# A router's load requests and its VectorE and ScalarE instructions put in one written order

## The chip, the cores and the metric

The kernel runs on one core of a Trainium2 chip. A core has TensorE (PE), VectorE (DVE), ScalarE (ACT), GpSimd (POOL) and SyncE (SP), each with an instruction queue of its own; SP issues nearly all of the loads here. The metric is the device time of one execution in microseconds (us), shown as the median of several runs.

## The reference, cut to what matters

One transformer block on 512 tokens of width 1024, in float32: a mixer (mLSTM and forgetting attention), a cross-attention on 256 memory rows, and a mixture of 32 experts in 4 groups, two experts for each token. Then a norm.

```python
x = x + merged @ w_out[l]
x = x + _cross_attention(_rmsnorm(x, g_xq[l]), _rmsnorm(mem, g_xmem[l]), w_xq[l], w_xkv[l], w_xo[l])
x = x + _hier_moe(_rmsnorm(x, g_moe[l]), w_rg[l], b_rg[l], w_re[l], b_re[l], w_gate[l], w_up[l], w_down[l])
```

Inside `_hier_moe` a token's logits pick a group and, in it, the best two experts; each expert is `silu(t @ w_gate) * (t @ w_up) @ w_down`, weighted and summed. The 32 experts hold 192 MiB of weights, all of which are read.

## The kernel before, in words

The change lies between the last attention head and the first pair of experts.

**w_xo.** The cross-attention's output product goes over four column blocks c of 256 columns. Each block needs two loads of 512 KB (`load_w`, L111 to L126): a request on SP into a buffer `wraw` (three of them), then a rounded high part `wh` on ACT (L124) and a rest `wl` on DVE (L125). Blocks 0 and 1 run in and right behind the last head (L642 to L657). Blocks 2 and 3 are `rw2` and `rw3` (L663); their four loads are the fifth to eighth of w_xo. A token block of theirs (`of_block`, L181) is 24 matmuls (12 with the first load, 12 with the second) and an add into the residual x (L525). In `ROUT` (L46), `x0` to `x3` are the token blocks of rw2 and `p0` to `p3` those of rw3.

**The router.** The other words of ROUT are its steps, the digit being a token block of 128 (or a half of two blocks for C, K and G): `t` transposes x on PE and copies it on ACT (L753), `l` multiplies it by the router's weights (L762), `s` and `r` sum squares on ACT (L766) and make the reciprocal root on DVE and POOL (L771, L772, L99), `Xh` and `Xl` write the high part of the scaled tokens on ACT (L780) and the low part on DVE (L782), `g` scales the logits (L788), `C` picks the experts on DVE (L797 to L818), `K` counts places with matmuls (L827) and then makes slots and hit tables on DVE (L830 to L837, L733, L734), and `G` gathers the first pair's tokens with matmuls (L883).

**The experts.** 16 pairs; for each, `stationary` gathers the tokens of 64 slots an expert (L1018, L1020), `gate_up` (L1043) multiplies by gate and up, `down` (L1067) by the third weight, `combine` (L1093, L1094) adds the results to x. The weights come in 192 pieces of 1 MB in a ring of 14 buffers (`RING`), nine of them named m; `h` and `l` take the places of `wh` and `wl`, and `r` lies in memory that is free when the router is done. `experts.load(n)` asks for all pieces up to n.

**What sets the order.** A scheduler orders each queue by a simulated clock. Inside `tc.manual_schedule(engines=...)` the instructions of the named engines keep the order in which they are written; those of other engines, and those of another such block, may be put between. In the kernel before, one block (L664) fixes PE, DVE and ACT from the loads of rw2 through the last word of ROUT. SP is in none. `experts.load(9)` stands behind the four loads of w_xo, and `experts.load(NAHEAD)` (11) at the word `v`. Behind that, PE is fixed in a block over all pairs (L1104); the two `st` tiles of the first pair (L1106) are in a DVE and ACT block of their own, and `codes`, `numbers` and `weight_parts` (the table of slots, the token numbers and the weights of the slots; L841 to L875, L964 to L978) in another (L1114).

Of the kernel before, what the change touches and what calls it, by code (L numbers as in the profile page):

```python
# [42 lines left out]
NAHEAD = 11  # L43


ROUT = ("x0 t00 t01 v s0 p0 l00 t02 s1 r0 x1 l01 t03 X0 p1 t10 l02 s2 r1 x2 l03 l10 t11 X1 s3 p2 l11 r2 g0 g1 C0 x3 t12 "  # L46
        "X2h K0 p3 X2l l12 t13 r3 l13 g2 g3 C1 G0 X3h K1 X3l G1")
NR = 8 + NE

C_MLQ, C_MLK, C_MLV, C_MLO = 0, 512, 1024, 2048  # L50
# [8 lines left out]
def emit(ctx, tc, a):  # L59
# [4 lines left out]
    dram = ctx.enter_context(tc.tile_pool(name="dram", bufs=1, space=bass.MemoryType.DRAM))  # L64
    accp = ctx.enter_context(tc.tile_pool(name="accp", bufs=4, space=PSUM))
    attp = ctx.enter_context(tc.tile_pool(name="attp", bufs=2, space=PSUM))
    small = ctx.enter_context(tc.tile_pool(name="small", bufs=8))
# [10 lines left out]
    def left(name, bufs=1):  # L78
        return tc.tile_pool(name=name, bufs=bufs, side="left", reuse_waits="tile")

    def right(name, bufs=1):
        return tc.tile_pool(name=name, bufs=bufs, side="right", reuse_waits="tile")


    ident = consts.tile([P, P], F32, name="ident")
# [21 lines left out]
    wp = None  # L107
# [20 lines left out]
    def drain(g):  # L128
        for _ in g:
            pass  # L130
# [97 lines left out]
    wp = ctx.enter_context(left("wp"))  # L228
# [269 lines left out]
    X1 = [X1a[:, tb] for tb in range(NB)]  # L498
# [17 lines left out]
    r2 = ExitStack()  # L516
# [5 lines left out]
    def resid_rows(src, hs, hl_, c):  # L522
        def ev(tb, n, ps):
            x = X1a[:, tb:tb + n, c * 256:(c + 1) * 256]
            V.tensor_add(x, x, ps)  # L525
        return Rows(src, c * 256, hs, hl_, NB, ev)
# [49 lines left out]
    with right("xa") as xa, tc.manual_schedule(engines={mybir.EngineType.PE}):  # L576
# [3 lines left out]
        def q_proj(hd, qs):  # L580
            def eq(i, ps):
                h = xa.tile([P, T], F32R, name="xqh", tag="xqh", bufs=4)
                l = xa.tile([P, T], F32R, name="xql", tag="xql", bufs=4)
                split(h, l, ps)
                qs.append((h, l))
            return proj_cols_g(a["w_xq"], hd * 256, xh, xl, T, eq)
# [51 lines left out]
        for hd in range(XA_H):  # L638
            nq = []
            if hd < XA_H - 1:  # L640
                g, per = q_proj(hd + 1, nq), 1
            else:  # L642
                def first_halves():
                    for c in range(2):
                        rows_o.append(resid_rows(a["w_xo"], oth, otl, c))
                        yield from rows_o[c].half(0)
                g, per = first_halves(), 2
# [12 lines left out]
    mraw = ctx.enter_context(right("mraw"))  # L660
    wx[:] = [0, s_ot.enter_context(left("wx"))]
    router, experts = moe(ctx, tc, a, X1, dram, small, acc, pss, pso, left, right, ident, rpow, wp, rt_, mraw, wx[1])
    rw2, rw3 = (resid_rows(a["w_xo"], oth, otl, c) for c in (2, 3))  # L663
    with tc.manual_schedule(engines={mybir.EngineType.PE, mybir.EngineType.DVE, mybir.EngineType.Activation}):  # L664
        rw2.loads()
        rw3.loads()
        experts.load(9)
        for w in ROUT.split():
            n = [int(x) if x.isdigit() else x for x in w[1:]]
            if w == "v":  # L670
                experts.load(NAHEAD)
            elif w[0] in "xp":
                drain((rw2 if w[0] == "x" else rw3).of_block(n[0]))
            else:
                router[w[0]](*n)
    s_ot.close()
    experts.run()


def router_consts(ctx, nc, a, left, gcol):  # L680
# [211 lines left out]
class Experts:  # L892
# [52 lines left out]
    def rows(self, e, w):  # L945
        return [*self.got[e, w, 0], *self.got[e, w, 1]]

    def run(self):
        self.mr2 = self.ctx.enter_context(self.right("mr2"))
        run_experts(self, *self.args)  # L950


def run_experts(ex, ctx, tc, a, X2, dram, small, acc, pss, pso, left, right, ident, rpow, wp, c, mraw):
    nc = tc.nc
    V, S, G, TE, SP = nc.vector, nc.scalar, nc.gpsimd, nc.tensor, nc.sync
    iot, iot64, Eb, Ab, rk, tokf, wsl = c.iot, c.iot64, c.Eb, c.Ab, c.rk, c.tokf, c.wsl
# [7 lines left out]
    def weight_parts():  # L964

        wpt = c.wparts
        dn = sg.tile([P, NB], F32, name="dn")
        V.scalar_tensor_tensor(dn, c.dv, 1.0, c.gs, op0=OP.add, op1=OP.mult)
        V.reciprocal(wf[:, :, 0], dn)
        V.tensor_mul(wf[:, :, 1], wf[:, :, 0], c.dv)  # L970
        rem = sg.tile([P, NB, 2], F32, name="rem")
        V.tensor_copy(wpt[:, :, :, 0], wf)
        V.tensor_sub(rem, wf, wpt[:, :, :, 0])
        V.tensor_copy(wpt[:, :, :, 1], rem)
        V.tensor_sub(rem, rem, wpt[:, :, :, 1])
        V.tensor_copy(wpt[:, :, :, 2], rem)
        V.tensor_mul(Vw, Eb.rearrange("p b j e -> p (b j) e")[:, :, None, :].to_broadcast([P, 2 * NB, 3, NE]),
                     wpt.rearrange("p b j a -> p (b j) a")[:, :, :, None].to_broadcast([P, 2 * NB, 3, NE]))  # L978
# [32 lines left out]
    def stationary(G_, g, n=P, pt=None):  # L1011

        st = sg.tile([P, 4, n], F32, name="st", tag="st", bufs=4)
        if pt is None:
            pt = pss()
            for j in range(4):
                for i in range(2 * NB):
                    TE.matmul(pt[:, j * n:(j + 1) * n], c.XN[:, i % 2, i // 2, (4 * g + j) * P:(4 * g + j + 1) * P],  # L1018
                              G_[:, i // 2, :n], start=i == 0, stop=i == 2 * NB - 1)
        V.tensor_mul(st, pt[:, :4 * n].rearrange("p (j t) -> p j t", j=4),  # L1020
                     c.gsc[:, 4 * g:4 * g + 4, None].to_broadcast([P, 4, n]))
        return st

    def slots_of(p):
        G_ = sg.tile([P, NB, P], F16, name="G", tag="G", bufs=2)
        for tb in range(NB):
            for i in range(2):
                e = 2 * p + i
                G.tensor_scalar(G_[:, tb, i * 64:i * 64 + 64], iot[:, :64], c.code[:, tb, e:e + 1], None,  # L1029
                                op0=OP.is_equal)  # L1030
        return G_
# [4 lines left out]
    def gate_up(sts, ws, ps):  # L1036


        for ph in range(2):
            for k in range(KB):  # L1040
                for h, w in enumerate(ws):
                    i = (ph + h) % 2
                    TE.matmul(ps[i][half(h)], sts[k // 4][:, k % 4, half(h)], w[i][k], start=k == 0, stop=k == KB - 1)  # L1043
                yield
# [36 lines left out]
    def places(tokcol, k=P):  # L1081
        C = sg.tile([P, T], F32R, name="C", tag="C", bufs=2)
        G.tensor_scalar(C[:k], iot[:k], tokcol, None, op0=OP.is_equal)
        return C
# [13 lines left out]
    def advance(g, n=99):  # L1098
        for _ in range(n):
            if g is None or next(g, "end") == "end":  # L1100
                return

    ex.load(len(ex.order))
    with tc.manual_schedule(engines={mybir.EngineType.PE}):  # L1104
        with tc.manual_schedule(engines={mybir.EngineType.DVE, mybir.EngineType.Activation}):
            sts = [stationary(c.G0, g, pt=c.pts[g]) for g in range(2)]  # L1106
        before = None
        for p in range(NPAIR):
            es = (2 * p, 2 * p + 1)
            ps = [acc(), acc()]  # L1110
            gu = gate_up(sts, [(ex.rows(e, 0), ex.rows(e, 1)) for e in es], ps)
            if p == 0:
                advance(gu, 6)
                with tc.manual_schedule(engines={mybir.EngineType.DVE, mybir.EngineType.Activation}):  # L1114
                    for f in (c.codes, c.numbers):
                        for h in range(2):
                            f(h)
                    weight_parts()
            if p + 1 < NPAIR:
                G_ = slots_of(p + 1)  # L1120
            C = places(tokf[:, p:p + 1])
            advance(gu, 4 if p else 2)
            cb = None
            if before:
                hT = turned(before[0], P)
            advance(gu, 4 if p else 0)
            if before:
                o = [pso(), pso()]
                advance(down(hT, [ex.rows(e, 2) for e in before[1]], o))
                cb = combine(*weigh(o, wsl[:, p - 1:p]), before[2])  # L1130
            advance(gu, 4)
            if p == 0:
                weights()
            if p == 1:
                nt, inc, nov = counts()
            nst = []
            if p + 1 < NPAIR:
                nst.append(stationary(G_, 0))
            advance(gu, 2)
            advance(cb, 4)  # L1140
            advance(gu, 2)
            if p + 1 < NPAIR:
                nst.append(stationary(G_, 1))
            advance(cb, 4)
            before = act(ps, P), es, C
            sts = nst
        hT = turned(before[0], P)
        o = [pso(), pso()]
        advance(down(hT, [ex.rows(e, 2) for e in before[1]], o))
        C = before[2]  # L1150
# [5 lines left out]
    with tc.If(n_ov > 0):  # L1156
        with left("ov") as ov:
# [4 lines left out]
            for tb in range(NB):  # L1162
                for j in range(2):
# [3 lines left out]
                    r1 = rk[:, tb, j:j + 1]  # L1167
# [42 lines left out]
            with tc.For_i(0, n_ov, 1) as it:  # L1210
                e = nc.values_load(ei[0:1, bass.ds(it, 1)], min_val=0, max_val=NE - 1,
                                   engines=[mybir.EngineType.SP])
# [17 lines left out]
    for tb in range(NB):  # L1230
# [3 lines left out]
        v = small.tile([P, 1], F32, name="vv", tag="vv")  # L1234
# [49 lines left out]
```

## Time and profile before

| | us |
|---|---|
| median of 3 runs (1303.69 to 1304.48) | 1303.83 |
| the profiled execution, its own time | 1306.05 |
| its span, first to last instruction | 1304.30 |
| mean granted clock of TensorE over the span | 0.988 |

Times in the rows are us from the start of the span. In a timeline a row is the start, the length, the engine, the line and operation, the tile written and those read, the shape and the count; in square brackets stands how long the engine was idle before it, and what ended that. SPq is SP's queue of requests. The length of a matmul is that of one pass through the pipeline, and matmuls overlap, so their rate is read from their starts. "x24" is a row of 24 instructions put together.

### The profile page before, as it was taken

How to read it: one execution, taken by the hardware profiler on the slowest of the kernel's cores; microseconds unless marked ns; L12 is line 12 of the kernel's file. 1: busy time of each engine (PE TensorE's matmuls, PEld its weight loads, DVE VectorE, ACT ScalarE, POOL GpSimd, SP SyncE). 2: the span in 40 equal slices, each digit the busy share in tenths (PEclk: the TensorE clock that was granted, in tenths of full speed). 3: DMA queues.
4: the chain of work that ended last, by engine and by line, in shares of the span. 5: the costliest groups of instructions: out<-in, count | busy, mean ns of one | idle time of the engine just before them, and what ended most of it. 6: DMA issues, size and time to landing. Idle time of an engine off the chain costs nothing.

```text
span 1304.3 us, 18633 instructions
## 1 busy us (share of the span) xinstructions
PE 1253.0 (96%) x7606; PEld 900.9 (69%) x7606; DVE 552.6 (42%) x1045; ACT 355.7 (27%) x627; POOL 132.3 (10%) x250
## 2 busy tenths in 40 slices
PE   6999999999999999999999986999999999999996
PEld 6898999888888977899978985444444444444443
DVE  4437455334566654446555516232323222222325
ACT  4435344222344442325434333000000000000102
POOL 0001011000001010001000003111112211111001
PEclk9999999999999999999999988999999999999998
DMA  4352422344344325233521444999999999999971
GB/s 167 85 111 82 81 90 74 96 97 89 89 86 84 88 82 159 83 130 120 178 81 50 191 164 180 403 417 418 419 417 418 418 418 414 417 417 416 418 326 66
DMA packets 99114, 278.45 MB, mean 213 GB/s; under 512 B 6197, under 2 KB 67909, under 8 KB 77905
## 3 DMA queue, kind: packets, MB, share of 16 engines
q1 hardware_dynamic: 97536, 272.46, 58.1%
q0 software_dynamic: 1488, 4.76, 1.1%
q8 instruction: 61, 1.00, 0.3%
q14 instruction: 29, 0.23, 0.1%
HBM read 275.08 MB, written 2.12 MB: 213 GB/s over the span
## 4 chain that ended last, share of the span: by engine, by line
PE 91%; DVE 4%; DMA 2%; ACT 1%; issue 1%; SPq 1%; POOL 0%; POOLq 0%; ACTq 0%; DVEq 0%
PE acc L1043 18%; PE acc L103 16%; PE acc L104 16%; PE acc L105 16%; PE pso L1067 8%; PE pss L1018 4%; PE pss L1093 1%; DMA wraw<-w_xo 1%; PE pso L1094 1%; PE pso L1093 1%; PE pss L103 1%; DVE wl L125 1%; PE pss L105 1%; PE pss L104 1%; PE pss L1056 1%
## 5 line engine op out<-in xcount | busy, mean ns | idle before, releaser
L1043 PE MATMUL acc<-mw,st 128*64 128x512 f32 x880 | 238.0, 604 | 0.4 <-DVE st L1020 0.4
L125 DVE TENSOR_TENSOR wl<-wraw,wh 128x1024 fp32r<-128x1024 f32 x120 | 146.9, 1224 | 193.7 <-ACT wh L124 189.1
L124 ACT ACTIVATE wh<-wraw 128x1024 fp32r<-128x1024 f32 x120 | 126.8, 1058 | 202.8 <-PE acc L104 93.2
L1043 PEld LDWEIGHTS acc<-mw,st 128*64 128x64 f32 x880 | 67.6, 138 | 109.7 <-issue 104.5
L103 PE MATMUL acc<-hH,wh 128*128 128x512 f32 x320 | 128.3, 401 | 0.0
L104 PE MATMUL acc<-hL,wh 128*128 128x512 f32 x320 | 127.8, 399 | 0.0
L105 PE MATMUL acc<-hH,wl 128*128 128x512 f32 x320 | 126.0, 401 | 1.7 <-DVE wl L125 1.7
L1078 DVE SCALAR_TENSOR_TENSOR yl<-pso,wsl,yh 128x512 fp32r<-128x512 f32 x32 | 22.5, 746 | 225.4 <-ACT yh L1077 225.4
L1067 PE MATMUL pso<-mw,hT 128*64 128x512 f32 x440 | 112.6, 592 | 0.7 <-ACT hT L1058 0.7
L104 PE MATMUL acc<-wl,hH 128*128 128x256 f32 x384 | 109.5, 286 | 1.1 <-DVE wl L125 1.1
L103 PE MATMUL acc<-wh,hH 128*128 128x256 f32 x384 | 109.6, 287 | 0.5 <-ACT wh L124 0.5
L105 PE MATMUL acc<-wh,hL 128*128 128x256 f32 x384 | 109.3, 285 | 0.2 <-DVE hL L196 0.2
L1029 POOL TENSOR_SCALAR G<-iot,code 128x64 f16<-128x64 f32 x120 | 52.9, 468 | 317.7 <-PE pss L1018 312.5
L1067 PEld LDWEIGHTS pso<-mw,hT 128*64 128x64 f32 x440 | 37.2, 137 | 61.4 <-issue 59.7
L104 PEld LDWEIGHTS acc<-wl,hH 128*128 128x128 f32 x384 | 73.3, 191 | 1.9 <-DVE wl L125 1.6
L103 PEld LDWEIGHTS acc<-wh,hH 128*128 128x128 f32 x384 | 73.0, 190 | 1.3 <-ACT wh L124 0.9
L105 PEld LDWEIGHTS acc<-wh,hL 128*128 128x128 f32 x384 | 73.5, 191 | 0.5 <-DVE hL L196 0.4
L105 PEld LDWEIGHTS acc<-hH,wl 128*128 128x128 f32 x320 | 60.8, 190 | 16.0 <-DVE wl L125 2.2
L103 PEld LDWEIGHTS acc<-hH,wh 128*128 128x128 f32 x320 | 60.6, 189 | 13.4 <-ACT wh L124 0.4
L104 PEld LDWEIGHTS acc<-hL,wh 128*128 128x128 f32 x320 | 60.6, 189 | 13.3
L1018 PEld LDWEIGHTS <-xn 128*128 128x128 f16 x960 | 53.7, 98 | 22.7 <-issue 22.7
L1077 ACT ACTIVATE yh<-pso,wsl 128x512 fp32r<-128x512 f32 x32 | 20.3, 684 | 154.3 <-PE pso L1067 154.3
(320 smaller groups left out, 2344.6 us busy)
## 6 DMA issues: line engine op xcount, KB each, us to landing
mw<-w_gate SPq DMA_DIRECT2D x55, 1024.0 KB, 13.7
mw<-w_up SPq DMA_DIRECT2D x55, 1024.0 KB, 12.8
mw<-w_down SPq DMA_DIRECT2D x55, 1024.0 KB, 11.0
wraw<-w_in SPq DMA_DIRECT2D x64, 512.0 KB, 5.5
wraw<-w_xkv SPq DMA_DIRECT2D x16, 512.0 KB, 3.4
mwl<-w_gate SPq DMA_DIRECT2D x10, 512.0 KB, 9.4
mwh<-w_up SPq DMA_DIRECT2D x10, 512.0 KB, 10.1
mwh<-w_down SPq DMA_DIRECT2D x10, 512.0 KB, 11.3
```

The lines of the kernel that those rows point to most:

```text
L103: TE.matmul(out, ah, bh, start=start, stop=False, **kw)
L104: TE.matmul(out, ah, bl, start=False, stop=False, **kw)
L105: TE.matmul(out, al, bh, start=False, stop=stop, **kw)
L124: S.activation(h, raw, AF.Copy)
L125: V.tensor_sub(l, raw, h.bitcast(F32))
L1018: TE.matmul(pt[:, j * n:(j + 1) * n], c.XN[:, i % 2, i // 2, (4 * g + j) * P:(4 * g + j + 1) * P], G_[:, i // 2, :n], start=i == 0, stop=i ...
L1029: G.tensor_scalar(G_[:, tb, i * 64:i * 64 + 64], iot[:, :64], c.code[:, tb, e:e + 1], None, op0=OP.is_equal)
L1043: TE.matmul(ps[i][half(h)], sts[k // 4][:, k % 4, half(h)], w[i][k], start=k == 0, stop=k == KB - 1)
L1067: TE.matmul(o[n][half(h)], hT[:, j, half(h)], w[j][:, n * 512:(n + 1) * 512], start=j == 0, stop=j == 3)
L1077: S.activation(yh[:k, c], o[n][:k], AF.Copy, scale=wcol)
L1078: V.scalar_tensor_tensor(yl[:k, c], o[n][:k], wcol, yh[:k, c].bitcast(F32), op0=OP.mult, op1=OP.subtract)
L1093: TE.matmul(o, C[:k, ts], yh[:k, c], start=True, stop=False)
```

## The change

Four things change. The requests of SP are fixed in a block of their own: the four loads of rw2 and rw3 first, then all of `experts.load(NAHEAD)`; the word `v` goes. DVE and ACT are held in one fixed block from the loads of w_xo through `weight_parts`, so that `codes`, `numbers` and `weight_parts` stand behind the two `st` tiles in both queues. PE is held in one block from there to the end of the pairs. In ROUT, `X2h` stands ahead of `g0 g1 C0` and so ahead of `t12`; `X2l` ahead of `K0`; `r3` ahead of `t13`; and `g2` ahead of `l13`.

```diff
-ROUT = ("x0 t00 t01 v s0 p0 l00 t02 s1 r0 x1 l01 t03 X0 p1 t10 l02 s2 r1 x2 l03 l10 t11 X1 s3 p2 l11 r2 g0 g1 C0 x3 t12 "
-        "X2h K0 p3 X2l l12 t13 r3 l13 g2 g3 C1 G0 X3h K1 X3l G1")
+ROUT = ("x0 t00 t01 s0 p0 l00 t02 s1 r0 x1 l01 t03 X0 p1 t10 l02 s2 r1 x2 l03 l10 t11 X1 s3 p2 l11 r2 X2h g0 g1 C0 x3 t12 "
+        "X2l K0 p3 l12 r3 t13 g2 l13 g3 C1 G0 X3h K1 X3l G1")
...
-    with tc.manual_schedule(engines={mybir.EngineType.PE, mybir.EngineType.DVE, mybir.EngineType.Activation}):
+    pe, both = ExitStack(), ExitStack()
+    pe.enter_context(tc.manual_schedule(engines={mybir.EngineType.PE}))
+    both.enter_context(tc.manual_schedule(engines={mybir.EngineType.DVE, mybir.EngineType.Activation}))
+    with tc.manual_schedule(engines={mybir.EngineType.SP}):
         rw2.loads()
         rw3.loads()
-        experts.load(9)
-        for w in ROUT.split():
-            n = [int(x) if x.isdigit() else x for x in w[1:]]
-            if w == "v":
-                experts.load(NAHEAD)
-            elif w[0] in "xp":
...
+        experts.load(NAHEAD)
+    for w in ROUT.split():
+        n = [int(x) if x.isdigit() else x for x in w[1:]]
+        if w[0] in "xp":
...
-    experts.run()
+    experts.run(pe, both)
...
-    with tc.manual_schedule(engines={mybir.EngineType.PE}):
-        with tc.manual_schedule(engines={mybir.EngineType.DVE, mybir.EngineType.Activation}):
-            sts = [stationary(c.G0, g, pt=c.pts[g]) for g in range(2)]
+    with pe:
+        sts = [stationary(c.G0, g, pt=c.pts[g]) for g in range(2)]
...
             if p == 0:
                 advance(gu, 6)
-                with tc.manual_schedule(engines={mybir.EngineType.DVE, mybir.EngineType.Activation}):
-                    for f in (c.codes, c.numbers):
-                        for h in range(2):
-                            f(h)
-                    weight_parts()
+                for f in (c.codes, c.numbers):
+                    for h in range(2):
+                        f(h)
+                weight_parts()
+                both.close()
```

## Rows read from the trace of the kernel before

**Rows 1.** Stretches: length; busy (count) of PE, PEld, DVE, ACT, POOL; clock, DMA share, GB/s
```profile
840.00:1240.00 400.00, 396.62 (x2382) 176.77 (x2378) 113.07 (x182) 33.26 (x54) 59.92 (x109) 1.00 1.01 417
...
764.00:766.00 2.00, 2.00 (x11) 2.00 (x11) 0.00 (x0) 0.92 (x2) 0.00 (x0) 0.50 0.01 4
770.00:786.00 16.00, 16.00 (x140) 16.00 (x140) 5.81 (x7) 8.78 (x13) 0.55 (x1) 1.00 0.00 1
```
**Rows 2.** Waits of SP's queue, 690 to 1300: who for whom, us, times, longest
```profile
SPq L929 <- PE acc L1043: 226.1, 52, 17.0
```
**Rows 3.** SP's requests in order of time
```profile
736.62 0.50 SPq L929 DMA_DIRECT2D mw<-w_gate  x1
...
844.41 0.33 SPq L929 DMA_DIRECT2D mw<-w_up  x1
```
**Rows 4.** The tile mw, 800 to 1290: from request to landing
```profile
DMA to landing us min/median/max: 6.4/11.8/16.8
```
**Rows 5.** The chain that ended last, in order of time
```profile
739.89 17.45 DMA wraw<-w_xo
...
808.26 7.53 PE acc L1043 x24
816.66 5.30 PE acc L1043 x24
...
874.68 3.43 PE acc L1043 x16
```
**Rows 6.** The eight requests of w_xo (L116, 679 to 770): to landing
```profile
DMA to landing us min/median/max: 3.4/3.8/17.4
```
**Rows 7.** PE in order of time
```profile
752.96 0.28 PE L104 MATMUL acc<-wl,oth 128*128 128x256 f32 x1
753.08 0.28 PE L105 MATMUL acc<-wh,otl 128*128 128x256 f32 x1
758.55 0.58 PE L103 MATMUL acc<-wh,oth 128*128 128x256 f32 x1 [5.19 <-ACT wh L124]
...
762.33 1.76 PE L762 MATMUL pso<-wr,rsc 128*128 128x40 f32 x8
...
769.18 0.98 PE L762 MATMUL pso<-wr,rsc 128*128 128x40 f32 x8
...
773.32 0.60 PE L750 MATMUL pss<-ident,x 128*128 128x128 f32 x4
...
803.62 2.72 PE L883 MATMUL pss<-G,xn 128*128 128x128 f16 x24 [3.22 <-DVE G L734]
806.87 1.04 PE L883 MATMUL pss<-G,xn 128*128 128x128 f16 x8 [0.52 <-DVE xn L782]
```
**Rows 8.** DVE in order of time
```profile
790.18 0.29 DVE L830 TENSOR_TENSOR jk<-eb,pso 128x128 f32<-128x128 bf16 x1
...
792.38 0.35 DVE L734 SCALAR_TENSOR_TENSOR G<-iot,cd,GA 128x128 f16<-128x128 f32 x1
793.12 0.42 DVE L525 TENSOR_TENSOR x<-x,acc 128x256 f32<-128x256 f32 x1 [0.40 <-PE acc L105]
793.46 2.08 DVE L782 SCALAR_TENSOR_TENSOR xn<-x,rpow,xn 128x1024 f16<-128x1024 f32 x1
...
796.80 0.26 DVE L788 SCALAR_TENSOR_TENSOR lg<-pso,rpow,br 128x40 f32<-128x40 f32 x1 [0.36 <-POOL rpow L99]
...
800.44 0.29 DVE L830 TENSOR_TENSOR jk<-eb,pso 128x128 f32<-128x128 bf16 x1 [0.37 <-PE pso L827]
...
804.76 2.05 DVE L782 SCALAR_TENSOR_TENSOR xn<-x,rpow,xn 128x1024 f16<-128x1024 f32 x1
```
**Rows 9.** ACT in order of time
```profile
787.40 2.12 ACT L780 ACTIVATE xn<-x,rpow 128x1024 f16<-128x1024 f32 x1
```
**Rows 10.** POOL in order of time
```profile
801.91 9.61 POOL L1029 TENSOR_SCALAR G<-iot,code 128x64 f16<-128x64 f32 x16 [5.14 <-DVE cd L837]
...
829.85 3.33 POOL L1029 TENSOR_SCALAR G<-iot,code 128x64 f16<-128x64 f32 x8 [9.49 <-PE pss L1018]
```

More of the change, by code (lines that the diff above doesn't have):

```diff
@@ L663, in emit @@
     rw2, rw3 = (resid_rows(a["w_xo"], oth, otl, c) for c in (2, 3))
-    with tc.manual_schedule(engines={mybir.EngineType.PE, mybir.EngineType.DVE, mybir.EngineType.Activation}):
+    pe, both = ExitStack(), ExitStack()
+    pe.enter_context(tc.manual_schedule(engines={mybir.EngineType.PE}))
+    both.enter_context(tc.manual_schedule(engines={mybir.EngineType.DVE, mybir.EngineType.Activation}))
+    with tc.manual_schedule(engines={mybir.EngineType.SP}):
         rw2.loads()
         rw3.loads()
-        experts.load(9)
-        for w in ROUT.split():
-            n = [int(x) if x.isdigit() else x for x in w[1:]]
-            if w == "v":
-                experts.load(NAHEAD)
-            elif w[0] in "xp":
-                drain((rw2 if w[0] == "x" else rw3).of_block(n[0]))
-            else:
-                router[w[0]](*n)
+        experts.load(NAHEAD)
+    for w in ROUT.split():
+        n = [int(x) if x.isdigit() else x for x in w[1:]]
+        if w[0] in "xp":
+            drain((rw2 if w[0] == "x" else rw3).of_block(n[0]))
+        else:
+            router[w[0]](*n)
     s_ot.close()
-    experts.run()
+    experts.run(pe, both)
 def router_consts(ctx, nc, a, left, gcol):
@@ L946, in rows, with run, run_experts @@
         return [*self.got[e, w, 0], *self.got[e, w, 1]]
-    def run(self):
+    def run(self, pe, both):
         self.mr2 = self.ctx.enter_context(self.right("mr2"))
-        run_experts(self, *self.args)
-def run_experts(ex, ctx, tc, a, X2, dram, small, acc, pss, pso, left, right, ident, rpow, wp, c, mraw):
+        run_experts(self, pe, both, *self.args)
+def run_experts(ex, pe, both, ctx, tc, a, X2, dram, small, acc, pss, pso, left, right, ident, rpow, wp, c, mraw):
     nc = tc.nc
```

## The prediction

> **What bounds the kernel now.** I read the stretches first, for the engine that is full. From 840 to 1240 us PE is busy for 396.62 of 400 us at the full clock, but the DMA share is 1.01 as well [rows 1], so that view alone can't say which of them sets the pace. The waits of SP's queue can: its requests wait 226.1 us for PE's gate and up matmuls to free a buffer [rows 2]. One piece as a check: requested at 844.41 [rows 3], first used at 874.68 [rows 5], some 30 us later, where the slowest piece takes 16.8 us to land [rows 4]. So a piece lies ready 13 us or more before its use, and loads follow PE. From the first expert matmul at 808.26 [rows 5] the rest is a PE stream, and I take the end to move with that start; I call it T0. What matters is then what holds T0 back, and for that I read the chain that ended last between 735 and 808.
>
> Its longest piece by far is the eighth load of w_xo: 17.45 us from 739.89 [rows 5], where the eight requests of w_xo have a median of 3.8 [rows 6]. The requests in order say why: from 736.62 on, expert pieces of 1 MB stand ahead of it in SP's queue [rows 3], and they share the DMA engines with it. PE shows the price: the first half of `p0` ends with the matmul at 753.08, the second half starts at 758.55 behind 5.19 us of idling [rows 7]. It is followed by a second price: at 764 to 766 the granted clock is 0.50, the lower of its two levels (1.2 GHz), and from 770 on 1.00 (2.4 GHz) [rows 1].
>
> **The change part by part.** *The eighth load.* Its buffer is freed by the rest `wl` of the fifth load, at about the time when it was requested before, so I leave the request at 739.9. With no expert piece ahead of it, it lands in between 3.4 us (the fastest of the eight) and 17.4 us (the slowest) [rows 6]; I take 3.8, since seven of the eight went out with no expert pieces in flight ahead of them. It is then there at 743.7, and needed shortly before 753.2; the 758.55 matmul started 1.2 us behind the landing at 757.34 [rows 5, 7]. Its parts `wh` and `wl` also need buffers that block 1 of w_xo frees before `x0` starts. So `p0` doesn't wait.
>
> What that is worth on PE: a next matmul would have started 0.12 us behind the one at 753.08, at 753.20 (the step between 752.96 and 753.08), and `p0` was over when the logits began at 762.33 [rows 7], 9.13 us later. Twelve matmuls at that step take 1.44. Gain 7.69 us. Then `l00 t02 x1` (8, 4 and 24 matmuls) took 762.33 to 769.18, 6.85 us, mostly at the lower clock; the same set `l01 t03 p1` took 769.18 to 773.32, 4.14 us [rows 7], at the upper one. Gain 2.71. Together **10.40 us**. From 770 to 786 PE is busy throughout [rows 1] and ACT and DVE follow it, so all of this stretch moves ahead by that.
>
> *The expert requests* move from 736.62 to about 740.3, 3.7 us later, behind w_xo's eighth. They cover the first nine pieces, which at 417 GB/s [rows 1] need some 23 us: there by about 764, and T0 is at 797. Cost nothing; the cover is over 30 us. The pieces in the places of `wh` and `wl` wait for the end of `p3` and the `r` pieces for the router's end as before, and both move with PE.
>
> *The exchanged steps*, in times of before (all of them move by 10.40). ACT: `X2h`, at 787.40 [rows 9], no longer has the copy of `t12` ahead of it, so it starts a little sooner and ends at 789.4; the copy is done at 790.0, and PE wants it only behind `p3`, which ends just ahead of the add at 793.12 [rows 8]: nothing. DVE: `X2l`, 2.08 us [rows 8], goes from behind the add of `p3` to ahead of `K0`. It starts at 790.1, so `K0` starts at 792.15 in place of 790.18. `K0` takes 2.55 us (790.18 to 792.38 and 0.35) and ends at 794.7; the add of `p3` behind it, at 793.12 before, comes at 794.6, 1.5 us later. `t13` on PE waits for that add (0.42) and starts 1.5 us later, at 795.2. Its transposes take 0.6 [rows 7], `r3`'s squares now go ahead of its copy on ACT, and the copy, of some 0.6, is done at 796.5; eight logits of 1.0 [rows 7] run to 797.6, and `g3`, at 796.80 before, comes at 797.65. It was later than its logits before because the 2.08 us of `X2l` at 793.46 [rows 8] held up the root of `r3`; that delay goes, so 1.5 us become 0.85. The exchange by itself is thus **0.85 us later** at `C1`.
>
> *codes and numbers behind st.* Between 800.44 and 804.76 DVE has `K1`, 4.32 us to `X3l` [rows 8], where `K0` needed 2.55: in between lie nine operations of codes and numbers. They go behind `st`. `K1` then starts at 801.3, `X3l` at 803.8 and ends at 805.8, 1.0 us ahead of before. The last eight matmuls of `G1`, at 806.87 [rows 7], start behind the 24 that wait for `K1`'s hit tables; those start at 803.3 in place of 803.62, and at the lower clock take 2.72 us [rows 7], to 806.0. So T0 gains **0.8 us** here, which PE and not `X3l` then limits.
>
> Behind T0 the moved work needs cover. The nine operations took 1.8 us there (4.32 less 2.55) and take at most 2.7 back to back (0.3 each); behind the two `st`, the second of which ends about 0.5 us after T0, that is T0 + 2.3 to 3.2. PE comes to the first matmul of numbers with 24 matmuls done, 5.3 us after T0 at the full clock and 7.5 at the lower [rows 5]. POOL's eight tables for pair 1 start at about T0 + 1.3, behind the first codes, and at 0.60 us each (9.61 for 16) end at T0 + 6; PE wants them behind the second 24 expert matmuls (816.66 and 5.30), T0 + 13.7 [rows 5, 10]. Cost nothing on both.
>
> A rule speaks against that. The row: POOL's comparisons take 0.60 us each at 801.91, with DVE at work beside them, and 0.42 at 829.85 [rows 10]. The Trainium skill, "SBUF — State Buffer", section "SBUF: two separate sides", says that a GpSimd operation and a VectorE one with two SBUF inputs shut each other out for a whole instruction. The slower POOL agrees. By that rule DVE's codes and tables, now beside POOL, would wait up to one POOL operation each. Worked from the rows: four such operations ahead of the first matmul of numbers, 0.42 each, give 1.7 us, T0 + 4.9 at most, still ahead of T0 + 5.3. So the sum is the same by both.
>
> **Sum.** 10.40 + 0.8 = 11.2 us. The profiled execution took 1306.05 (span 1304.30 and 1.75 around it), 2.2 above the median of the runs, 1303.83. So 1294.8 for it, and **1292.6 us** for the median.
>
> **The rivals.** *A, the clock falls sooner or longer.* PE idles 1.5 us more at `t13`, near other waits. At the lower clock `l13` is 1.0 us longer and T0 moves by as much; and if the first 24 expert matmuls all run at the lower clock, they take twice 5.30, 10.6, in place of 7.53, which already is a mixture [rows 5]. 1293.6 to 1296.7. For it, that 7.53: the clock does fall in the router. Against it, the new wait is shorter than the 5.19 us behind which the clock fell at 758. *B, the clock doesn't fall at T0*, since the waits ahead of it get shorter: 24 matmuls in 5.30 and not in 7.53 [rows 5], 2.2 us more, 1290.4. *C, the loads set the end.* For it, the DMA share of 1.01; against it, 13 us of lead and SP's waits. Then nothing moves: 1303.8. *D, the change doesn't do what it says*: the eighth load still lands late, because its buffer, not its place, held it. Then 0.8 us is left: 1303.0. Against it: it was requested at 739.89 and took 17.45 us. *E, slower*: the code table behind `st` is late, and PE waits for pair 1's tables in front of its first `stationary`. The price decides only when the tables come later than T0 + 13.7 + 11.2, at T0 + 24.9; to lose 2.6 us they must come at T0 + 27.5. With all 16 of POOL at 0.60 they end at T0 + 11, so over 16 us of unknown delay would be needed; that gives 1306.5.
>
> **How the numbers follow.** The forecast has 0.66; A 0.15, B 0.10, C 0.03, D 0.03, E 0.03. A measurement of this kernel can tell about 0.2%, 2.6 us, from no change. Faster by more: forecast, A and B, 0.91; within it C and D, 0.06; slower E, 0.03. The range goes from B with 0.9 us for a cheaper exchange, 1289.5, to A with 0.3 on top, 1297.0; C, D and E lie outside of it.
>
> **What would show it.** The longest landing of w_xo falls from 17.4 to under 6 us; no wait over 1 us in `p0`; the clock 1.00 from 740 to 785; the first expert matmul near 797; `X2l` ahead of `K0`'s tables, and `t13` starting 1.5 us behind the end of `l12`; DVE's codes behind both `st`, and no wait of PE for them; 30 us from pair to pair as before. It is wrong if pieces of the experts land just ahead of their use, if PE waits for numbers or for G, or if the eighth w_xo lands late all the same.

## The result, and the profile after

| | before | after |
|---|---|---|
| median of 5 runs each, on the same chip | 1304.48 (1303.69 to 1309.03) | 1292.79 (1292.05 to 1294.51) |
| ratio, with its 95% interval | | 0.9904 (0.9885 to 0.9924) |
| the profiled execution | 1306.05 | 1293.15 |
| its span | 1304.30 | 1291.30 |
| mean granted clock | 0.988 | 0.993 |

The changed kernel is faster by 0.96%. The span is 13.0 us shorter. The lines below answer to those shown of before.

SP's requests in order of time, and then the landings, first of the eight w_xo requests, then of the tile mw from 790 to 1290:

```profile
735.84 3.56 SPq L116 DMA_DIRECT2D wraw<-w_xo  x2
739.46 0.50 SPq L930 DMA_DIRECT2D mw<-w_gate  x1
```
```profile
DMA to landing us min/median/max: 3.3/3.5/4.0
...
DMA to landing us min/median/max: 7.2/12.7/17.5
```

The first expert request now stands behind the eighth w_xo request. The longest landing of w_xo is 4.0 us instead of 17.4 [rows 6].

PE in order of time:

```profile
754.38 0.98 PE L763 MATMUL pso<-wr,rsc 128*128 128x40 f32 x8
...
758.53 0.98 PE L763 MATMUL pso<-wr,rsc 128*128 128x40 f32 x8
...
779.25 0.18 PE L828 MATMUL pso<-ab,before 128*128 128x32 bf16 x1 [3.05 <-DVE ab L819]
...
784.46 0.44 PE L751 MATMUL pss<-ident,x 128*128 128x128 f32 x2 [0.97 <-DVE x L525]
785.90 1.06 PE L763 MATMUL pso<-wr,rsc 128*128 128x40 f32 x8 [1.01 <-DVE lg L789]
...
792.68 3.60 PE L884 MATMUL pss<-G,xn 128*128 128x128 f16 x32 [2.01 <-DVE G L735]
...
803.40 0.35 PE L863 MATMUL acc<-Vj,R 128*128 128x32 f16 x4 [0.33 <-DVE Vj L861]
```

`p0` runs through without a wait, so its first logits come at 754.38 (762.33 before [rows 7]) and take 0.98 in place of 1.76. From there to the logits of `l01` it is 4.15 us (6.85 before). The line at 792.68 is all 32 matmuls of `G1`: their one wait is for the hit tables, and none is for `X3l`, which held up the last eight before [rows 7].

The stretches (length; busy and count of PE, PEld, DVE, ACT, POOL; clock, DMA share, GB/s) and the chain:

```profile
744.00:786.00 42.00, 36.96 (x318) 36.34 (x317) 19.59 (x55) 17.29 (x28) 2.48 (x5) 1.00 0.59 238
790.00:798.00 8.00, 5.24 (x41) 3.94 (x42) 6.55 (x19) 2.53 (x9) 0.00 (x0) 0.60 0.91 381
840.00:1240.00 400.00, 396.36 (x2396) 178.59 (x2396) 115.13 (x179) 32.58 (x53) 60.30 (x110) 1.00 1.01 417
```
```profile
796.64 6.23 PE acc L1044 x24
```

The clock stays at 1.00 where it was 0.50 before, at 764 to 766 [rows 1]. It still falls ahead of the experts (0.60 over 790 to 798), but most of the first 24 expert matmuls run at full speed: 6.23 us, not 7.53 [rows 5]. The stream behind them is as it was: PE busy for 396.36 of 400 us, and SP's requests still waiting 213.4 us for PE (226.1 [rows 2]):

```profile
SPq L930 <- PE acc L1044: 213.4, 52, 13.2
```

Where the 13.0 us come from, in order of time: 0.35 were there ahead of `x0` already (the matmul that ends the block of w_xo before it starts at 737.59, in place of 737.94); 7.60 up to `l00`; 2.70 from `l00` to `l01`; 0.97 from `l01` to the first expert matmul T0 (38.11 us, in place of 39.08). T0 is thus 11.62 sooner, 796.64 in place of 808.26. Another 1.30 come from the first 24 expert matmuls, and 0.08 from all the rest.

DVE around the exchanged steps and behind `st`, and POOL:

```profile
779.45 2.22 DVE L783 SCALAR_TENSOR_TENSOR xn<-x,rpow,xn 128x1024 f16<-128x1024 f32 x1
...
783.99 0.41 DVE L525 TENSOR_TENSOR x<-x,acc 128x256 f32<-128x256 f32 x1
787.07 0.26 DVE L789 SCALAR_TENSOR_TENSOR lg<-pso,rpow,br 128x40 f32<-128x40 f32 x1 [1.31 <-PE pso L763]
790.71 0.29 DVE L831 TENSOR_TENSOR jk<-eb,pso 128x128 f32<-128x128 bf16 x1 [0.37 <-PE pso L828]
793.13 2.06 DVE L783 SCALAR_TENSOR_TENSOR xn<-x,rpow,xn 128x1024 f16<-128x1024 f32 x1
...
797.10 0.16 DVE L847 TENSOR_SCALAR rf<-rk 128x4 f32<-128x4 f32 x1
...
799.39 0.68 DVE L855 TENSOR_TENSOR R<-iot,rk 128x512 f16<-128x512 f32 x1
```
```profile
798.05 7.75 POOL L1030 TENSOR_SCALAR G<-iot,code 128x64 f16<-128x64 f32 x16 [11.74 <-DVE rf L847]
```

`X2l` (779.45) is ahead of `K0`. `K1` takes 2.42 us to `X3l` (790.71 to 793.13), 4.32 before [rows 8]. Codes start at 797.10, behind both `st`, and POOL's 16 tables end 9.2 us behind T0, so rival E has no ground. The moved operations end at 800.07 (799.39 and 0.68), 3.4 us behind T0, where 2.3 to 3.2 were forecast; PE comes to the first matmul of numbers at 802.80, 6.2 us behind T0. The only wait for numbers is the 0.33 us at 803.40, for the second half, whose `Vj` reuses the buffer of the first. The kernel before has the same wait:

```profile
816.32 0.35 PE L862 MATMUL acc<-Vj,R 128*128 128x32 f16 x4 [0.33 <-DVE Vj L860]
```

### The profile page after: what moved, and what is told of

Its sections match the earlier page's. It is cut to its first block, busy times and chain, and to the rows that moved or that the text cites. A ratio compares the mean times of both kernels' runs of the same rounds, so it can differ in the third digit from the quotient of the medians.

```text
span 1291.3 us, 18633 instructions
## 1 busy us (share of the span) xinstructions
PE 1247.0 (97%) x7606; PEld 896.2 (69%) x7606; DVE 552.9 (43%) x1045; ACT 355.8 (28%) x627; POOL 130.5 (10%) x250
## 4 chain that ended last, share of the span: by engine, by line
PE 93%; DVE 3%; ACT 1%; issue 1%; DMA 1%; SPq 0%; POOL 0%; POOLq 0%; DVEq 0%; ACTq 0%
PE acc L1044 18%; PE acc L103 16%; PE acc L105 16%; PE acc L104 16%; PE pso L1068 9%; PE pss L1019 4%; PE pss L1094 1%; PE pso L1095 1%; PE pso L1094 1%; PE pss L103 1%; PE pss L105 1%; PE pss L104 1%; PE pss L1057 1%; PE pss L1095 1%; DVE st L1021 1%
```

## Experiments

Ten kernels. "Eighth load" is the request of the eighth w_xo load and its landing; "l00" the first logits; "first 24" what the first 24 expert matmuls take. The stretches at the lower clock (0.50) are given by where they start and how long they last. The requests are fixed as in the changed kernel in all but e2, e5, e6 and e7. Medians in us; e5 and e6 ran once. Each ratio is to runs of the kernel before on the same chip, whose medians are 1304.12 to 1305.70 us; the columns from "eighth load" on are from one profiled execution of each kernel.

| kernel | median | ratio (interval) | eighth load | l00 | T0 | l00 to T0 | first 24 | lower clock |
|---|---|---|---|---|---|---|---|---|
| before | | 1 | 739.89, 757.34 | 762.33 | 808.26 | 45.93 | 7.53 | 758.0, 10.2; 802.4, 10.2 |
| after | 1292.79 | 0.9904 (0.9885 to 0.9924) | 739.04, 742.53 | 754.38 | 796.64 | 42.26 | 6.23 | 791.6, 6.8 |
| e1 | 1295.41 | 0.9925 (0.9908 to 0.9941) | 739.08, 742.42 | 754.30 | 797.51 | 43.21 | 7.36 | 791.3, 10.2 |
| e2 | 1303.91 | 0.9984 (0.9975 to 0.9994) | 739.83, 757.82 | 762.80 | 807.63 | 44.83 | 6.24 | 758.2, 10.2; 802.6, 6.8 |
| e3 | 1291.00 | 0.9899 (0.9883 to 0.9916) | 738.96, 742.35 | 754.18 | 795.48 | 41.30 | 5.37 | 791.4, 3.4 |
| e4 | 1295.64 | 0.9921 (0.9904 to 0.9937) | 739.11, 742.49 | 754.34 | 798.46 | 44.12 | 6.92 | 791.4, 10.2 |
| e5 | 1294.03 | one run | 737.25, 750.35 | 754.23 | 796.54 | 42.31 | 7.31 | 780.0, 3.4; 793.7, 6.8 |
| e6 | 1300.37 | one run | 738.42, 754.06 | 759.05 | 804.46 | 45.41 | 5.37 | 756.0, 10.2; 786.7, 3.4; 800.4, 3.4 |
| e7 | 1299.50 | 0.9959 (0.9945 to 0.9973) | 739.35, 757.24 | 761.11 | 804.23 | 43.12 | 5.37 | 784.9, 6.8 |
| e8 | 1289.64 | 0.9885 (0.9869 to 0.9902) | 738.55, 741.93 | 753.77 | 794.01 | 40.24 | 5.37 | 787.2, 6.8 |
| e9 | 1290.06 | 0.9881 (0.9864 to 0.9897) | 739.84, 743.22 | 755.18 | 795.20 | 40.02 | 5.37 | none |
| e10 | 1289.18 | 0.9874 (0.9858 to 0.9891) | 739.01, 742.31 | 754.24 | 793.83 | 39.59 | 5.37 | none |

**e1 and e2: which half of the change does it?** e1 is the kernel before with SP's block alone; PE, DVE and ACT keep their order. e2 is the changed kernel without that block.

```diff
(e1, in the kernel before)
+        with tc.manual_schedule(engines={mybir.EngineType.SP}):
+            rw2.loads()
+            rw3.loads()
+            experts.load(NAHEAD)
...
(e2, in the changed kernel)
-    with tc.manual_schedule(engines={mybir.EngineType.SP}):
-        rw2.loads()
-        rw3.loads()
-        experts.load(NAHEAD)
+    rw2.loads()
+    rw3.loads()
+    experts.load(NAHEAD)
```

> The kernel before with SP's requests alone put in a fixed order (the four loads of rw2 and rw3, then eleven expert pieces); steps, and codes and numbers, as before. Theory (the eighth load is late because expert pieces stand ahead of it): longest landing of w_xo under 6 us, no wait in p0, clock 1.00 from 744 to 786, first expert matmul (T0) 10.4 us sooner than before, so 10 to 11 us off the time. Rival 1 (its buffer held it, not its place): landing and T0 as before, no change of time. Rival 2 (the fixed order of VectorE and ScalarE brings most of it): under 5 us.

> The changed kernel without the fixed block of SP's requests, so that the eighth w_xo load stands behind six expert pieces again; the new steps and the one order of VectorE and ScalarE stay. Theory: landing of about 17 us, a wait of some 5 us in p0 and the lower clock behind it come back; T0 only 0.8 us sooner than before, the time within 2.6 us of before. Rival (the fixed order of VectorE and ScalarE brings most of it): over 5 us faster than before.

PE of e2, then the landings of its eight w_xo requests:

```profile
759.03 0.58 PE L103 MATMUL acc<-wh,oth 128*128 128x256 f32 x1 [5.51 <-ACT wh L124]
762.80 1.76 PE L762 MATMUL pso<-wr,rsc 128*128 128x40 f32 x8
```
```profile
DMA to landing us min/median/max: 3.4/3.5/18.0
```

With the order of the engines changed and that of the requests not, the eighth load takes 18.0 us again, PE waits 5.51 for it and the slow logits are back; 0.16% of gain is left. With the requests alone, 0.75% is there: e1 has the landings of the changed kernel and its l00 within 0.1 us. The spans add up: e1 is 11.0 us shorter than before, e2 2.0, both parts together 13.0. Rival D, that its buffer held the load, falls, and C with it, since the end moved with T0.

**e3 and e4: the two parts of the second half.** e3 is the changed kernel with the old step order; e4 is the kernel before with SP's block (as in e1) and the new order, so that codes, numbers and weight_parts, and the blocks of the engines, stay as they were.

```diff
(e3, in the changed kernel)
-"... X2h g0 g1 C0 x3 t12 X2l K0 p3 l12 r3 t13 g2 l13 g3 ..."
+"... g0 g1 C0 x3 t12 X2h K0 p3 X2l l12 t13 r3 l13 g2 g3 ..."
...
(e4, in the kernel before, beside SP's block)
-"... g0 g1 C0 x3 t12 X2h K0 p3 X2l l12 t13 r3 l13 g2 g3 ..."
+"... X2h g0 g1 C0 x3 t12 X2l K0 p3 l12 r3 t13 g2 l13 g3 ..."
```

> The changed kernel with the steps of ROUT in their old order (without the word v); requests fixed, codes and numbers behind st. Theory (exchanging X2l costs 0.85 us at C1, moving codes gains 1.8 at K1): T0 about 0.85 us sooner than in the changed kernel, so 0 to 1 us faster than it. Rival (the exchange of the steps is a gain of its own): T0 later than in the changed kernel by 0.5 us or more.

> The changed kernel with codes, numbers and weight_parts in a block of their own again, so that nine of their operations lie between K1's; requests fixed, new steps. Theory: K1 on VectorE takes 4.3 us to X3l in place of 2.4 and T0 is 1.5 to 1.9 us later than in the changed kernel. Rival (G1 on TensorE and not X3l sets T0): T0 within 0.3 us of the changed kernel.

From l00 to T0 the four kernels make a square: e1 has neither part (43.21), e4 the steps (44.12), e3 the codes (41.30), the changed kernel both (42.26). So the exchange costs 0.91 or 0.96 us, and codes behind `st` (with the blocks of the engines joined, as the change has them) give 1.91 or 1.86, whichever way round one goes. DVE of e3:

```profile
785.91 0.26 DVE L789 SCALAR_TENSOR_TENSOR lg<-pso,rpow,br 128x40 f32<-128x40 f32 x1 [0.36 <-POOL rpow L99]
```

With the old steps `g3` waits for the root of `r3`, as the prediction read it, and comes 31.73 us behind l00; with the new ones it waits for `l13` (787.07) and comes 32.69 behind. In the changed kernel `l13` itself waits 1.01 us for `g2`, which reads the logits of `l12` and now stands behind the root of `r3`: a link that the prediction did not have. It costs only some 0.2 us: the copy of `t13` on ACT, which `l13` needs as well, ends at 785.64 (785.06 and 0.58), and `l13` starts at 785.90, 0.26 behind it; in e3 it starts 0.05 behind. DVE of e4 shows what the codes cost in their old place:

```profile
790.64 0.29 DVE L829 TENSOR_TENSOR jk<-eb,pso 128x128 f32<-128x128 bf16 x1 [0.37 <-PE pso L826]
...
794.97 2.04 DVE L781 SCALAR_TENSOR_TENSOR xn<-x,rpow,xn 128x1024 f16<-128x1024 f32 x1
```

That is 4.33 us from `K1` to `X3l`, 2.42 with the codes behind `st`. The whole time of e3 has the lower median, by 1.8 us, but the two ratios' intervals overlap; the square in the traces, not the times, carries the 0.9.

**e5 and e6: how many expert pieces may stand ahead of the eighth load?** Four and five, in place of none.

```diff
-        rw3.loads()
+        rw3.ws = [rw3.load(0)]
+        experts.load(4)        (e6: 5)
+        rw3.ws.append(rw3.load(4))
         experts.load(NAHEAD)
```

> The changed kernel with four expert pieces put ahead of the eighth w_xo load (none in the changed kernel, six in the one before). Theory (the queue is worked off in order, 2.5 us for a piece of 1 MB): it lands at about 751.5, the high part is ready at 752.6 and the low part at 753.9, against 753.2 when PE comes to it: a wait of 0.3 to 1.5 us in p0, the clock stays at 1.00, T0 within 1.5 us of the changed kernel. Rival (any expert piece ahead costs the whole 10 us): a wait over 3 us.

> The same with five pieces ahead. Theory: landing at about 754, PE waits 2.5 to 3.5 us in p0. If the lower clock follows only a longer wait, T0 is about 3 us later than in the changed kernel; if it follows this one too, 6 to 7 us later.

PE of e5 and its stretch from 760 to 766, then the same two of e6:

```profile
752.83 0.38 PE L104 MATMUL acc<-wl,oth 128*128 128x256 f32 x1 [0.88 <-DVE wl L125]
```
```profile
760.00:766.00 6.00, 6.00 (x54) 6.00 (x53) 2.50 (x2) 4.64 (x7) 0.00 (x0) 1.00 0.14 57
```
```profile
755.28 0.38 PE L103 MATMUL acc<-wh,oth 128*128 128x256 f32 x1 [2.89 <-ACT wh L124]
```
```profile
760.00:766.00 6.00, 6.00 (x30) 6.00 (x31) 0.36 (x2) 1.81 (x5) 0.55 (x1) 0.50 0.34 141
```

From request to landing the load takes 3.5 us with none ahead, 13.1 with four, 15.6 with five and 17.4 to 18.0 with six (before, e2 and e7). That is 1.8 to 2.5 us more for each piece, and 1 MB at the 417 GB/s [rows 1] is 2.5 us. It lands behind all that was requested before it: in the kernel before, the expert pieces requested on either side of it, at 739.37 and 740.32, landed at 755.91 and 759.84, and it at 757.34. The Trainium skill, "DMA: Bandwidth & Descriptors", section "Queues, rings and completion order", says that each DMA engine takes the descriptors of a queue in ring order; the landings agree. The cost is a step, not a slope: four pieces cost nothing at T0 (796.54 against 796.64; the first 24 matmuls behind it then took 1.08 longer), the fifth 7.9 us (7.8 over the changed kernel, where 6 to 7 were expected; each ran once). Up to l00 it is 4.8 later than with four, through the wait of 2.89 in `p0` and the matmuls behind it at the lower clock, and from `l00` to `l01` it takes 7.40 us in place of 4.14, at the lower clock, which came in with these two waits and not with the single 0.88 of e5.

**e7: the clock apart from the wait.** e2, with 46 matmuls that nobody reads put into the wait of `p0` (e9 and e10 below have such matmuls too, 44 of them).

```diff
+            g = (rw2 if w[0] == "x" else rw3).of_block(n[0])
+            if w == "p0":
+                for _ in range(4):
+                    next(g)
+                idle = pso()
+                for i in range(46):
+                    TE.matmul(idle[:, :256], oth[0][:, :P], oth[0][:, :256], start=i == 0, stop=i == 45)
+            drain(g)
```

> The changed kernel without the fixed requests (eighth load late, wait of 5.5 us in p0), and 46 additional matmuls on data that is there, whose result nobody reads, put on PE into that wait, ahead of the second half of p0; some 5.5 us of work at the full clock. Theory (of the 10.4 us the wait itself is about 6.5, and 3.9 is what the matmuls behind it lose at the lower clock): landing late as before, but the clock is 1.00 from 752 to 786 and T0 3.5 to 4 us sooner than without the additional matmuls, the time about 1300. Rival (the matmuls behind the wait are slow for another reason, or the additional ones delay p0): T0 within 1 us or later.

PE of e7, and its stretch from 760 to 766 (e2's has 27 matmuls at 0.50):

```profile
761.11 0.98 PE L769 MATMUL pso<-wr,rsc 128*128 128x40 f32 x8
765.26 0.98 PE L769 MATMUL pso<-wr,rsc 128*128 128x40 f32 x8
```
```profile
760.00:766.00 6.00, 6.00 (x55) 6.00 (x55) 1.21 (x4) 1.82 (x5) 0.55 (x1) 1.00 0.45 187
```

The load still lands at 757.24 and the set from `l00` to `l01` takes 4.15 us, as in the changed kernel (6.73 in e2). By `l01` PE is 4.27 us ahead of e2; 0.87 of it is given back in the router, where the lower clock begins at 784.9 (it was expected to stay at 1.00 to 786), so T0 is 3.40 us sooner, just under the 3.5 to 4 expected. So a late load costs twice, as the prediction had it: by the idling, and by the lower clock behind it, and the second can be bought back without the first.

**e8, e9 and e10: what is left ahead of T0?** e8 orders the steps a third way, against the 3.05 us that PE waits ahead of `K0`: the low part of X1 and of X2 go where DVE waits for PE. e9 adds 18 and 26 matmuls that nobody reads ahead of `K1` and `G1`; e10 splits the last `X3l` in two halves as well.

```diff
(e8, in the changed kernel)
-"... t11 X1 s3 p2 l11 r2 X2h g0 g1 C0 x3 t12 X2l K0 p3 l12 r3 t13 g2 l13 g3 C1 G0 X3h K1 X3l G1"
+"... t11 X1h s3 p2 l11 g0 g1 C0 r2 x3 t12 X2h K0 p3 l12 r3 t13 X1l l13 g2 g3 C1 X2l G0 X3h K1 X3l G1"
...
(e9, in e8)
-"... X3h K1 X3l G1"
+"... X3h f18 K1 X3l f26 G1"
+        if w[0] == "f":
+            idle, n = acc(), int(w[1:])
+            for i in range(n):
+                TE.matmul(idle[:, :256], rt_.XN[:, 0, 0, :P], rt_.XN[:, 0, 0, :256], start=i == 0, stop=i == n - 1)
...
(e10, in e9)
-            V.scalar_tensor_tensor(xl, xv, sq[tb][:, 0:1], xh, op0=OP.mult, op1=OP.subtract)
+            for j in ((slice(0, 4), slice(4, 8)) if tb == 3 else (slice(0, 8),)):
+                V.scalar_tensor_tensor(xl[:, j], xv[:, j], sq[tb][:, 0:1], xh[:, j], op0=OP.mult, op1=OP.subtract)
```

> Requests fixed, codes behind st, and the steps in a third order: the adds and the choice of block pair 0 (p2, g0, g1, C0) ahead of X1l and of r2, K0 with no X*l ahead of it, X1l behind t13's root, X2l between C1 and K1. Theory (PE's wait of 3.05 us at K0 is VectorE's X1l ahead of C0; behind it VectorE is the bound up to X3l): the wait at K0 falls under 0.5 us, X3l ends 0.5 to 1 us sooner than with the old steps, T0 0.5 to 1.5 us sooner than there, the time 1289.5 to 1290.5. Rival (the wait only moves, to K1 and G1): T0 within 0.3 us of the old steps or later.

> The third order of steps (X1l and X2l out of the way of C0 and K0), and additional matmuls whose result nobody reads in PE's waits of the router: 18 ahead of K1, 26 ahead of G1, about 0.11 us each. Theory (the lower clock at G1 and at the first expert matmuls is what PE's idling at K1 and G1 brings on): the clock stays at 1.00 from there through T0, the first 24 expert matmuls take 5.3 us in place of 6.4, T0 0.2 to 0.4 us sooner than without them; together 1.2 to 1.6 us off the time of the third order, 1288.0 to 1288.6. Rival (the additional matmuls delay K1 or G1 themselves): T0 later by 0.5 us or more and no gain.

> The same, with X3l on VectorE in two operations of half the width, so that the first st follows X3l without waiting for PE's last matmuls of its half. Theory: T0 0.3 to 0.5 us sooner than with one operation. Rival (PE's pass over G1 or VectorE's additional start takes it back): T0 within 0.1 us.

PE of e8, its stretch from 790 to 794 and its chain; then the same three of e9:

```profile
775.74 0.18 PE L828 MATMUL pso<-ab,before 128*128 128x32 bf16 x1 [0.16 <-DVE ab L819]
786.28 0.18 PE L828 MATMUL pso<-ab,before 128*128 128x32 bf16 x1 [2.48 <-DVE ab L819]
790.06 3.60 PE L884 MATMUL pss<-G,xn 128*128 128x128 f16 x32 [3.51 <-DVE G L735]
```
```profile
790.00:794.00 4.00, 3.60 (x32) 3.22 (x31) 3.26 (x6) 0.00 (x0) 0.00 (x0) 0.50 0.91 383
```
```profile
794.01 5.37 PE acc L1044 x24
```
```profile
794.02 0.62 PE L888 MATMUL pss<-G,xn 128*128 128x128 f16 x8 [1.06 <-DVE xn L787]
```
```profile
790.00:794.00 4.00, 2.28 (x32) 1.88 (x29) 3.75 (x9) 0.59 (x1) 0.00 (x0) 1.00 1.00 422
```
```profile
795.20 5.37 PE acc L1048 x24
```

e8 takes the wait ahead of `K0` from 3.05 to 0.16. Part of it comes back at `K1` (2.48, 1.60 in the changed kernel) and at `G1` (3.51, 2.01); from l00 to T0 it is 2.02 us shorter than the changed kernel and 1.06 shorter than e3. e9 is a miss. Its clock is 1.00 all through, yet l00 to T0 falls by 0.22 us and the time not at all, where 1.2 to 1.6 us were expected. In e8 the clock is back at T0 already: its first 24 expert matmuls take 5.37 us, as in e9, so there was nothing to buy back there; and the gather, faster at the full clock, now waits 1.06 us for `X3l`, the bound that the slow gather had hidden. e10 goes at that: its T0 is 0.43 us nearer to l00 than in e9. Its median, 1289.18 us, is the lowest of all, but its ratio's interval overlaps those of e8 and e9. The three beat the kernel before by 1.2%. Their medians lie 2.7 to 3.6 us under that of the changed kernel, but on other chips, and the intervals of their ratios overlap its own. So the times do not show that they beat it; the traces show 2.0 to 2.7 us less from l00 to T0.

## Why the prediction was right, and where it was off

**The eighth load** (7.69 predicted): 7.60 measured, with the landing 3.5 us after the request (3.8 taken). e2 shows that this is the order of the requests and nothing else, e5 and e6 that it is their place in the queue. **The slow logits behind it** (2.71): 2.70, and e7 shows by itself that they are the clock's. **The expert requests later** (nothing): they came 2.8 us later (739.46), not 3.7, and the stream behind T0 is unchanged. Tables don't hold it up, and numbers no more than before: PE's 0.33 us of waiting for them, a sign of being wrong by the prediction's own list, is in the kernel before too.

**The exchange** (0.85 later): 0.91 and 0.96. The add of `p3` holds up `t13` (0.97 on PE), and the root of `r3` no longer waits for `X2l`, as predicted. The wait of `l13` for `g2` is the link that it lacked, worth some 0.2; the other steps came some 0.1 sooner than forecast. **Codes behind `st`**: `K1` 1.90 us shorter, 1.8 predicted; `G1` is then limited by PE, as predicted. The two together were to give 0.8 and gave 0.95 (e1 against the changed kernel, l00 to T0). On DVE beside POOL: POOL's 16 tables took 7.75 us beside the codes, 9.61 before [rows 10], and the two wide tables of numbers on DVE 0.68 each, in both kernels with POOL at work beside them. Here the 1.7 us that the prediction worked out for the Trainium skill's rule ("SBUF — State Buffer", "SBUF: two separate sides") did not show.

**The step that was mis-sized** is the clock at T0. The sum let the first 24 expert matmuls take 7.53 us as before and put the other cases into the rivals, all at the lower clock (A) or all at the upper one (B). The run took 6.23, between the forecast and B, and 1.30 us more than the 11.2 were gained; A's way, a longer stretch from the wait at `t13`, did not come. The table shows how these times come about: they are 5.37 and half of what is left of the stretch at the lower clock when T0 comes. In the changed kernel the stretch ends at 798.4, 1.8 us behind T0, and 6.23 is 0.86 over 5.37; before it ends at 812.6, 4.3 behind T0, and 7.53 is 2.16 over; in e1 4.0 are left (1.99 over), in e4 3.1 (1.55), in e3 and e8 none. The sum had carried the 4.3 over unchanged, where the changed router starts its stretch 5.0 us ahead of T0 (5.9 before) and has it for 6.8 us (10.2 before). In the profiled executions the stretch was shorter in e2, e3 and after, which have codes behind `st`, and not in e1 and e4, which do not. That this is the cause is not shown, and other executions put it in doubt: the mean granted clock is 0.995 in e4's shortest (1292.94 us) and 0.991 or 0.992 in its others, and 0.990 in e3's longest (1294.53 us) and 0.995 in its others. So one kernel can spend more or less time at the lower clock, and a single trace does not settle the size of this term.

The forecast of 1292.6 us lies 0.2 under the median, and part of that is luck. For the profiled execution the sum gave 1294.8, and 1293.15 came, 1.65 sooner, nearly all of it the 0.35 from ahead of `x0` and the 1.30 from the first 24 matmuls. The profiled execution of before stood 2.2 us over the median of three that the forecast started from, that of after 0.4 over its own median; so two differences of nearly the same size cancelled.

## What to carry to other kernels

Where a small load stands in one queue with a large prefetch, count the bytes requested ahead of it: it lands after all of them, and there is slack up to the piece that makes it late, then a step. A wait of PE can cost twice, by its idling and by the matmuls behind it at the lower clock; read the second from the same set of matmuls at the other clock elsewhere in the trace, and leave room for both cases, since waits of 3 us brought the lower clock in some of these kernels and not in others. Work that only the steady part needs belongs behind the first instruction of that part, and an exchange that frees one engine is to be followed through every buffer that the next step shares.

## What was not expected of the hardware

The length of a stretch at the lower clock did not follow the wait ahead of it: 10.2 us behind 5.19 us of idling in `p0` (before), and the same 10.2 with waits of only 2.89 and 0.88 (e6), in both from a point before the last wait was over; none behind 0.88 alone (e5). The wait ahead of `K0` is 3.00 to 3.09 us in all kernels from before to e7: the clock stayed at 1.00 there in before, after and e1 to e4, and fell in e5 and e6 (3.4 us each) and e7 (6.8). Ahead of the experts it was 6.8 us with PE waiting 1.60 and 2.01 (the changed kernel), 3.4 with 2.16 and 2.01 (e3), 6.8 with 2.48 and 3.51 (e8). What decides whether the clock falls behind such waits, and for how long, stays open. It was worth as much as the order of the steps: e3 and the changed kernel differ by 0.96 us from l00 to T0, and by 0.86 more in the first 24 expert matmuls.
